# Seven block products for eight in the gated unit and the output projection of a hybrid attention and state-space layer

## The chip, the cores and the metric

The kernel runs on one core of a Trainium2 chip. Its engines are TensorE (PE in the rows; PEld is its loading of weights), VectorE (DVE), ScalarE (ACT), GpSimd (POOL) and SyncE (SP), which here does nothing but issue DMAs. The metric is the device time of one launch in microseconds, as the median of several executions; one further execution was taken with the hardware profiler, and all rows below are from that one.

## What is computed

One layer of an encoder, 1024 tokens of width 2048, all in fp32. The part in question stands in the middle (cut from the reference; `y_attn`, `y_ssm`, `gate_s` come from the input projection, attention and the scan):

```
y_ssm = gelu(y_ssm)
glu   = y_ssm @ w_glu + b_glu                      # 1024 x 1024 by 1024 x 2048
y_ssm = glu[..., :1024] * sigmoid(glu[..., 1024:]) * silu(gate_s)
h     = x + concatenate([y_attn, y_ssm]) @ w_out   # 1024 x 2048 by 2048 x 2048
gate  = sigmoid(rms_norm(h) @ w_ple_gate)          # 2048 x 2048
h     = h + gate * (p @ w_ple_proj)
out   = rms_norm(h)
```

## The kernel before

All matrices lie with channels on the 128 partitions and tokens along the free axis. Every fp32 product is made of three matmuls: each operand is split into a high part H (rounded to fp32r, by ACT) and a low part L (what the rounding left, by DVE), and H H + H L + L H is summed in PSUM. `split` does that (L307 on ACT, L308 on DVE; with a gain L310 and L311), `split_pool` does both on POOL.

The stages follow each other on PE: the input projection with the scan of the state-space part beside it (to 966 us), attention (to 1219), and then `back`, once for each half of 512 tokens. A half consists of the gated unit (names `gv`, `gg`: 8 pairs of output tiles, 8 blocks of input channels each), the output projection (`ph`: 16 tiles by 16 blocks) and the gate with the projection of p (`pg`: 16 by 16, `pp`: 16 by 2). `mm_half` issues the three matmuls of a block, 128 x 128 weights by 128 x 512 tokens. Its weights come four blocks at a time: `w_dma` loads 128 x 512 into `wraw` (3 buffers) on SP's queue, `w_split` splits it into `wH` and `wL` (4 buffers), and `w_next` keeps this two groups ahead of PE. All weights of `back` are loaded and split twice, once for each half.

The order on each engine is the order in which the program writes the instructions; nothing is reordered. What has to run beside the matmuls is written as a generator and put into `bgs`; each `tick` (after every second block) lets every generator go one step. So `fin_glu` (L1094 to L1096) evacuates a pair of tiles, `fin_h` (L1105 to L1116) adds x to a tile of the projection, splits it at once as an operand of the gate, and adds its square to `xsq`, on POOL (L1114). Operands of a stage are kept split in SBUF, in tiles of 128 x 2 x 512 from the pool `big` (33 buffers).

Of the kernel before, what the change touches and what calls it, by code (L numbers as in the profile page):

```python
# [16 lines left out]
SEQ = 1024  # L17
# [221 lines left out]
class Kernel:  # L239
# [10 lines left out]
    def __init__(self, ctx, tc, ins, out):  # L250
# [13 lines left out]
        self.bgs = []  # L264
# [5 lines left out]
    def tick(self):  # L270
        for g in list(self.bgs):
            try:
                next(g)
            except StopIteration:
                self.bgs.remove(g)

    def drain(self):
        while self.bgs:
            self.tick()
# [79 lines left out]
    def w_plan(self):  # L359
# [10 lines left out]
        for kind, n in self.order[2:]:  # L370
            tile_(w_in[self.COL[kind] + n], KD)
        for _ in range(2):
            for n in range(8):
                tile_(self.i["w_glu"][n], 8)
                tile_(self.i["w_glu"][n + 8], 8)
            for n in range(16):
                tile_(self.i["w_out"][n], 16)
# [22 lines left out]
    def w_next(self):  # L400
        n = self.wi
        while len(self.w_raw) < min(n + self.W_DMA + 1, len(self.wq)):
# [3 lines left out]
        while len(self.w_hl) < min(n + self.W_SPLIT + 1, len(self.wq)):  # L406
            self.w_split()
# [3 lines left out]
        return r  # L411

# [28 lines left out]
    def scratch(self):  # L441
# [11 lines left out]
        self.d_h = [[d(f"d_h{f}_{n}", (128, 512)) for n in range(KD)] for f in range(2)]  # L453
# [449 lines left out]
    def attn_scores(self, b):  # L903
        nc, sm = self.nc, self.sp
# [117 lines left out]

    def mm_half(self, ps, nk, xs):

        nc = self.nc
        for k in range(nk):
            if k % 4 == 0:
                H, L = self.w_next()
            while k not in xs:
                assert self.bgs  # L1030
                self.tick()
            x = xs[k]
            nc.tensor.matmul(ps, H[:, k % 4], x[:, 0], start=(k == 0), stop=False)  # L1033
            nc.tensor.matmul(ps, H[:, k % 4], x[:, 1], start=False, stop=False)  # L1034
            nc.tensor.matmul(ps, L[:, k % 4], x[:, 0], start=False, stop=(k == nk - 1))  # L1035
# [3 lines left out]
    def y_load(self, hf, js=range(8)):  # L1039
        raw = []  # L1040
        for j in js:
            t = self.cyc()
            self.nc.sync.dma_start(
                t.rearrange("p (t c) -> p t c", t=4),
                self.d_y[j][4 - 4 * hf : 8 - 4 * hf].rearrange("t f c -> f t c"),
            )
            raw.append(t)
        return raw

    def y_gelu(self, raw):  # L1050
        for t in raw:
            self.nc.scalar.activation(t, t, AF.Gelu_apprx_tanh)

    def y_first(self, raw):
        for _ in range(8):
            yield
        self.y_gelu(raw)

    def y_split(self, hf, raw, yg, j0=0, pool=False):
# [356 lines left out]
```

## Time and profile before

| | us |
|---|---|
| median of three runs | 2173.71 (2167.40 to 2174.03) |
| profiled execution, its own time | 2165.21 |
| its span, first to last instruction | 2163.3 |
| TensorE busy | 2112.9 |
| VectorE busy | 1358.0 |
| ScalarE busy | 787.9 |
| GpSimd busy | 618.1 |

The profiled execution lies 8.5 us under the median of the runs, and 1.9 us of its time lie outside the span. Busy times of PE are modelled from pipelined matmuls, so they are to be read with the starts of the matmuls beside them.

### The profile page before, as it was taken

The numbers are of one execution on the slowest core, as the hardware profiler recorded it, in microseconds if no ns is written. First come the engines' busy times: TensorE is split into PE (matmuls) and PEld (weight loads), VectorE is DVE, ScalarE is ACT, GpSimd is POOL, SyncE is SP. The second block draws the span as 40 slices with busy tenths as digits, with TensorE's granted clock in tenths as the row PEclk, the third lists the DMA queues.
The fourth block names the chain that finished last, engine by engine and source line by source line (L and its number), as shares of the span: only waits on it lengthen the run. The fifth ranks groups of instructions, "written<-read, shape, count | busy, mean of one in ns | idle before, by whom it ended". The sixth has DMA issues, their size and how long they took to land.

```text
span 2163.3 us, 29094 instructions
## 1 busy us (share of the span) xinstructions
PE 2112.9 (98%) x10428; PEld 1765.6 (82%) x10428; DVE 1358.0 (63%) x2274; ACT 787.9 (36%) x1429; POOL 618.1 (29%) x605
## 2 busy tenths in 40 slices
PE   8999999999999999999999999999999999999996
PEld 6888878888878887778989888888888788888885
DVE  7654787778888787838999644444444744444334
ACT  7111322222222222337777633333335433333332
POOL 0143456555556565502113000111121001111122
PEclk9999999999999999999999999999999999999998
DMA  6323233332332332341111334444434744443333
GB/s 215 96 95 102 81 87 101 90 94 86 95 99 77 88 105 72 100 157 65 70 41 40 122 122 137 145 154 122 125 122 144 235 128 145 146 152 109 128 113 126
DMA packets 171151, 245.06 MB, mean 113 GB/s; under 512 B 27136, under 2 KB 77440, under 8 KB 170752
## 3 DMA queue, kind: packets, MB, share of 16 engines
q1 hardware_dynamic: 169856, 241.12, 35.9%
q10 hardware_dynamic: 1152, 2.10, 0.3%
q8 instruction: 82, 1.34, 0.2%
q14 instruction: 61, 0.50, 0.1%
HBM read 189.35 MB, written 48.56 MB: 110 GB/s over the span
## 4 chain that ended last, share of the span: by engine, by line
PE 50%; DVE 3%; ACT 1%; issue 1%; DMA 1%; POOL 0%; DVEq 0%; SPq 0%; ACTq 0%
PE ph L1035 5%; PE ph L1033 5%; PE ph L1034 5%; PE pg L1035 5%; PE pg L1033 5%; PE pg L1034 5%; PE ptr L943 2%; PE pv L956 1%; PE pv L957 1%; PE pv L958 1%; PE S L913 1%; PE gg L1035 1%; PE S L916 1%; PE S L912 1%; PE gg L1033 1%; PE gg L1034 1%
## 5 line engine op out<-in xcount | busy, mean ns | idle before, releaser
L308 DVE TENSOR_TENSOR wL<-wraw,wH 128x512 fp32r<-128x512 f32 (+1 forms) x496 | 402.6, 832 | 445.3 <-ACT wH L307 440.0
L307 ACT CAST wH<-wraw 128x512 fp32r<-128x512 f32 (+1 forms) x496 | 292.7, 604 | 443.5 <-PE ph L1034 125.8
L1033 PE MATMUL pg<-hg,wH 128*128 128x512 f32 x512 | 200.3, 391 | 0.0
L1035 PE MATMUL pg<-hg,wL 128*128 128x512 f32 x512 | 199.5, 390 | 0.6 <-DVE wL L308 0.6
L1034 PE MATMUL pg<-hg,wH 128*128 128x512 f32 x512 | 199.2, 389 | 0.0
L1114 POOL TENSOR_TENSOR xsq<-xsq,tz 128x512 f32<-128x512 f32 x30 | 39.0, 1301 | 515.9 <-ACT tz L1113 515.9
L825 ACT COPY ks<-kp 16x224 f32<-16x224 f32 x32 | 10.7, 336 | 341.7 <-DVE ks L824 189.4
L1035 PEld LDWEIGHTS pg<-hg,wL 128*128 128x128 f32 x512 | 96.1, 188 | 21.4 <-DVE wL L308 1.3
L1034 PEld LDWEIGHTS pg<-hg,wH 128*128 128x128 f32 x512 | 96.1, 188 | 20.5 <-issue 0.5
L1033 PEld LDWEIGHTS pg<-hg,wH 128*128 128x128 f32 x512 | 96.1, 188 | 20.1 <-issue 0.5
L507 PE MATMUL zga<-hH,wH 128*128 128x512 f32 x256 | 104.0, 406 | 0.0
L507 PE MATMUL zgs<-hH,wH 128*128 128x512 f32 x256 | 102.5, 401 | 0.7 <-ACT wH L307 0.7
L507 PE MATMUL zq<-hH,wH 128*128 128x512 f32 x256 | 102.9, 402 | 0.0
L508 PE MATMUL zga<-hL,wH 128*128 128x512 f32 x256 | 100.2, 392 | 0.0
L508 PE MATMUL zq<-hL,wH 128*128 128x512 f32 x256 | 100.2, 391 | 0.0
L508 PE MATMUL zgs<-hL,wH 128*128 128x512 f32 x256 | 100.0, 391 | 0.0
L1033 PE MATMUL ph<-ma,wH 128*128 128x512 f32 x256 | 99.6, 389 | 0.0
L1034 PE MATMUL ph<-ma,wH 128*128 128x512 f32 x256 | 99.6, 389 | 0.0
L1035 PE MATMUL ph<-ma,wL 128*128 128x512 f32 x256 | 99.6, 389 | 0.0
L1033 PE MATMUL ph<-ms,wH 128*128 128x512 f32 x256 | 99.6, 389 | 0.0
L1034 PE MATMUL ph<-ms,wH 128*128 128x512 f32 x256 | 99.6, 389 | 0.0
L1035 PE MATMUL ph<-ms,wL 128*128 128x512 f32 x256 | 99.6, 389 | 0.0
(420 smaller groups left out, 5356.0 us busy)
## 6 DMA issues: line engine op xcount, KB each, us to landing
wraw<-in_w_in_dram SPq DMA_DIRECT2D x144, 256.0 KB
wraw<-in_w_out_dram SPq DMA_DIRECT2D x128, 256.0 KB
wraw<-in_w_gate_dram SPq DMA_DIRECT2D x128, 256.0 KB
wraw<-in_w_glu_dram SPq DMA_DIRECT2D x64, 256.0 KB
xraw<-in_xT_dram SPq DMA_DIRECT2D x15, 512.0 KB
out_dram<-h SPq DMA_DIRECT2D x24, 256.0 KB
t<-zz SPq DMA_DIRECT2D x40, 128.0 KB
d_u<-tz SPq DMA_DIRECT2D x16, 256.0 KB
```

Of the source, the lines that this page charges most:

```text
L307: nc.scalar.copy(H, src)
L308: nc.vector.tensor_tensor(L, src, H.bitcast(F32), ALU.subtract)
L507: nc.tensor.matmul(ps[h], H[:, kk, :], rH[:, s], start=(k == 0), stop=False)
L508: nc.tensor.matmul(ps[h], H[:, kk, :], rL[:, s], start=False, stop=False)
L912: nc.tensor.matmul(S[:, s], qH[:, qs], kH[:, s], start=True, stop=False)
L913: nc.tensor.matmul(S[:, s], qH[:, qs], kL[:, s], start=False, stop=False)
L916: nc.tensor.matmul(S[:, s], qL[:, qs], kH[:, s], start=False, stop=True)
L943: nc.tensor.transpose(pc[:, b], P[:, 512 * hf + 128 * b : 512 * hf + 128 * b + 128], self.ident)
L1033: nc.tensor.matmul(ps, H[:, k % 4], x[:, 0], start=(k == 0), stop=False)
L1034: nc.tensor.matmul(ps, H[:, k % 4], x[:, 1], start=False, stop=False)
L1035: nc.tensor.matmul(ps, L[:, k % 4], x[:, 0], start=False, stop=(k == nk - 1))
L1114: nc.gpsimd.tensor_tensor(acc, acc, s2, ALU.add)
```

## The change

The gated unit, the attention half of the output projection (its first 1024 input channels) and the state-space half become three stages of their own, each over all 1024 tokens. In each, the 1024 input channels are cut in two, the tokens in two, and the output tiles are taken in pairs: a 2 x 2 by 2 x 2 block product, done with Strassen's seven products in Winograd's order of sums. A stage is 8 units (`unit`), one for each pair of output tiles; a unit is 7 products of 4 blocks of 128 channels, each 3 matmuls, so 84 matmuls of the same shape as before. Each product has a PSUM tile of its own (`pr`) and is closed after 12 matmuls.

- Weights: a unit loads its four blocks once (`sw_dma`, `sraw`, 6 buffers), makes four sums of them on POOL (`sw_sum`, L436) and splits seven operands (`sw_prep`), two products ahead.
- Token operands: a stage has 7 sets of 4 tiles. Four sets are sums, made on POOL by `t_make` (16 operations a stage) and stored to DRAM (`d_t`): for the first stage in attention, for the second from the second unit of the first stage on, for the third from the first unit of the second stage on. `put` loads each tile raw into the slot of its own low part, and `fill` splits it in place some ticks later, one tile a tick. The 28 tiles of a next stage are loaded and split in the last unit of a stage and the first of the next, as products of that last unit free their slots.
- Evacuation: `u_glu` and `u_out` combine the seven products in fp32, with DVE reading PSUM and POOL adding to the token-wide tiles `cx`. The gated result goes to DRAM (`d_ms`), the partial sum of the projection too (`d_p`), and h (`d_h`), from which `put_h` loads the operands of the gate and splits them with the gain.
- GELU is applied to whole channels ahead of attention and stored (`y_prep`, `d_y2`). The gate stage itself keeps its matmuls; both of its halves now follow each other. `xsq`, the sum of squares of h, is 1024 wide, and the sums for the last norm move to other tiles.

The core of the diff:

```diff
-        while len(self.w_hl) < min(n + self.W_SPLIT + 1, len(self.wq)):
+        while len(self.w_hl) < min(n + self.W_SPLIT + 1, self.w_end):
+    def sw_sum(self, u, o, a, b, op):
+        if o not in self.sr and isinstance(o[1], str):
+            self.sr[o] = self.wp.tile([128, 512], F32, name="wraw", tag="wraw", bufs=3)
+        self.nc.gpsimd.tensor_tensor(self.sr[o], self.sr[a], self.sr[b], op)
+    def sw_prep(self, g):
+        u, i = divmod(g, 7)
...
+        src = (A11, A12, S2, A11, S1, A12, A22)[i]
...
+        self.split(H, L, self.sr[src].rearrange("p (k m) -> p k m", m=128))
+        self.shl[g] = (H, L)
+        if i == 0:
+            self.sw_dma(u + 1, (0, 1))
+        elif i == 1:
+            self.sw_sum(u, S1, A21, A22, ALU.add)
+            self.sw_sum(u, S2, S1, A11, ALU.subtract)
+        elif i == 2:
+            self.sw_sum(u, A11, A11, A21, ALU.subtract)
...
+        elif i == 3:
...
+            self.sw_sum(u, A12, A12, S2, ALU.subtract)
...
+        elif i == 4:
...
+            self.sw_dma(u + 1, (2, 3))
...
+    def sw_next(self):
+        g = self.sg
+        self.sg += 1
+        for j in range(g, g + 3):
+            if j not in self.shl:
+                self.sw_prep(j)
+        return self.shl.pop(g)
...
+    def put(self, X, key, src, gain=None, pool=False, wait=6):
+        x = self.hl("st")
+        self.nc.sync.dma_start(x[:, 1].bitcast(F32), src)
+        self.fq.append((self.nt + wait, X, key, x, gain, pool))
...
+    def unit(self, X, thread, hook):
+        nc = self.nc
+        next(thread)
+        for i in range(7):
+            H, L = self.sw_next()
+            ps = self.psC("pr")
+            for k in range(4):
+                while (i, k) not in X:
+                    assert self.fq
+                    self.tick()
+                x = X[i, k]
+                nc.tensor.matmul(ps, H[:, k], x[0], start=(k == 0), stop=False)
+                nc.tensor.matmul(ps, H[:, k], x[1], start=False, stop=False)
+                nc.tensor.matmul(ps, L[:, k], x[0], start=False, stop=(k == 3))
+                self.tick()
+            thread.send(ps)
+            hook(i)
...
+    def u_out(self, m, src, dst, sq):
...
+        ps = yield
+        u1 = self.t2k("tz")
+        nc.scalar.copy(u1, ps)
+        add(r[0], h0, u1)
+        ps = yield
+        done(r[0], h0, ps)
+        ps = yield
+        nc.vector.tensor_tensor(u1, ps, u1, ALU.add)
+        ps = yield
+        u2 = self.t2k("tz")
+        nc.vector.tensor_tensor(u2, ps, u1, ALU.add)
+        add(r[1], h1, u2)
+        add(r[1], h0, u2)
+        ps = yield
+        nc.vector.tensor_tensor(u1, ps, u1, ALU.add)
+        add(r[0], h1, u1)
+        done(r[1], h1, ps)
+        ps = yield
+        done(r[0], h1, ps)
...
+        ps = yield
+        done(r[1], h0, ps)
...
```

In it `add` is a sum on POOL, and `done` one on DVE from PSUM, with the square on ACT and its sum on POOL where the third stage needs them.

How the instructions stand on DVE where one stage passes into the next. Before, at the first tiles of the projection (`ph`) of a half; x4 means four in a row:

```order
L308 TENSOR_TENSOR ms_7_12660<-tz,ms_7_12660 128x512
L308 TENSOR_TENSOR wL<-wraw,wH 128x512 x4
L1105 TENSOR_TENSOR r_12636<-ph,r_12636 128x512
L311 SCALAR_TENSOR_TENSOR hg_0_12733<-r_12636,vec,hg_0_12733 128x512
L308 TENSOR_TENSOR wL<-wraw,wH 128x512 x4
L1105 TENSOR_TENSOR vr<-ph,vr 128x512
```

Now, in the last unit of the first stage, from its third product on (`st` are tiles of the next stage, split in place; `pr` is a product in PSUM):

```order
L311 TENSOR_TENSOR wL<-sraw,wH 128x512
L311 TENSOR_TENSOR st<-st 128x512 x4
L1209 TENSOR_TENSOR tz<-pr,tz 128x512
L311 TENSOR_TENSOR wL<-sraw,wH 128x512
L311 TENSOR_TENSOR st<-st 128x512 x4
L1212 TENSOR_TENSOR tq<-pr,tz 128x512
L1213 SCALAR_TENSOR_TENSOR tz<-pr,vec,tz 128x512
L311 TENSOR_TENSOR wL<-sraw,wH 128x512
L311 TENSOR_TENSOR st<-st 128x512 x4
L1217 TENSOR_TENSOR tz<-pr,tz 128x512
L1218 TENSOR_TENSOR cx<-tz,tq 128x512
L311 TENSOR_TENSOR wL<-sraw,wH 128x512
```

Where a weight split stood behind other weight splits and one operation on a finished tile, it now stands behind four splits of the next stage's tiles in each product.

On POOL, the projection before has one operation in a tile of 48 matmuls; the rows around it are those of the gate, ahead of it and behind it:

```order
L1151 TENSOR_TENSOR xsq<-xsq,tq 128x512
L1140 TENSOR_TENSOR h_14_15385<-tab,tz 128x512
L1114 TENSOR_TENSOR xsq<-xsq,tz 128x512 x15
L1140 TENSOR_TENSOR h_0_17674<-W,tz 128x512
L1140 TENSOR_TENSOR h_0_17674<-tab,tz 128x512
```

Now, one unit of the third stage (84 matmuls) on POOL, from the weight sums for it on (`sraw`, `wraw` are weights and their sums, `cx` the tiles of h):

```order
L436 TENSOR_TENSOR wraw<-sraw 128x512
L436 TENSOR_TENSOR wraw<-wraw,sraw 128x512
L1254 TENSOR_TENSOR xsq<-xsq,tq 128x512
L436 TENSOR_TENSOR sraw<-sraw 128x512
L1242 TENSOR_TENSOR cx<-cx,tz 128x512
L436 TENSOR_TENSOR sraw<-sraw,wraw 128x512
L1254 TENSOR_TENSOR xsq<-xsq,tq 128x512
L1242 TENSOR_TENSOR cx<-cx,tz 128x512 x3
L1254 TENSOR_TENSOR xsq<-xsq,tq 128x512 x2
```

The fifteen sums of a half's projection, one in 10.9 us, become twelve in every unit, and four of them stand between a load and a weight split.

## Rows read from the trace of the kernel before

**Rows 1.** The page, parts 1 and 2: busy us, share, instructions; tenths in 40 slices.
```profile
PE 2112.9 (98%) x10428; PEld 1765.6 (82%) x10428; DVE 1358.0 (63%) x2274; ACT 787.9 (36%) x1429; POOL 618.1 (29%) x605
...
ACT  7111322222222222337777633333335433333332
...
PEclk9999999999999999999999999999999999999998
```

**Rows 2.** Windows by stage; the first row names the columns.
```profile
core 0: us, PE busy (x) PEld busy (x) DVE busy (x) ACT busy (x) POOL busy (x), PEclk, DMA share, GB/s
...
100.00:740.00 640.00, 634.61 (x3191) 529.31 (x3190) 467.89 (x791) 151.72 (x342) 343.07 (x353) 1.00 0.31 93
740.00:1218.70 478.70, 461.34 (x2764) 399.76 (x2763) 387.46 (x684) 253.41 (x463) 148.35 (x141) 1.00 0.24 76
1218.70:1305.70 87.00, 87.00 (x387) 72.05 (x386) 41.59 (x63) 33.25 (x55) 0.00 (x0) 1.00 0.49 158
1305.70:1479.80 174.10, 174.10 (x770) 144.16 (x769) 78.33 (x99) 58.97 (x98) 18.21 (x14) 1.00 0.47 146
...
1672.00:1763.60 91.60, 90.61 (x401) 74.12 (x400) 56.45 (x92) 37.25 (x64) 3.89 (x3) 1.00 0.57 187
1763.60:1937.00 173.40, 173.40 (x767) 143.58 (x766) 78.53 (x99) 58.98 (x98) 18.22 (x14) 1.00 0.48 148
```

**Rows 3.** Tiles gv and ph, first half: ns min/median/max, first and last start.
```profile
L1033 PE MATMUL gv<-yg,wH x64: 389/389/396, 1218.8 to 1299.8; 128*128 128x512 f32 x64
...
L1033 PE MATMUL ph<-ma,wH x128: 389/389/389, 1305.9 to 1473.9; 128*128 128x512 f32 x128
...
L1035 PE MATMUL ph<-ms,wL x128: 389/389/389, 1311.8 to 1479.8; 128*128 128x512 f32 x128
```

**Rows 4.** Lines 308, 307, 1105, 1113 (1305.7 to 1479.8), 1114; DVE's 311 from 1218.
```profile
L308 DVE TENSOR_TENSOR wL<-wraw,wH x64: 677/693/1451, 1309.6 to 1477.9; 128x512 fp32r<-128x512 f32 x64
...
L307 ACT CAST wH<-wraw x64: 602/622/623, 1308.9 to 1477.3; 128x512 fp32r<-128x512 f32 x64
...
L1105 DVE TENSOR_TENSOR W<-ph,W x4: 691/692/692, 1349.6 to 1458.4; 128x512 f32<-128x512 f32 x4
...
L1113 ACT ACTIVATE tz<-W x4: 616/616/618, 1351.0 to 1459.8; 128x512 f32<-128x512 f32 x4
...
L1114 POOL TENSOR_TENSOR xsq<-xsq,tz x30: 1290/1297/1338, 1330.0 to 1945.6; 128x512 f32<-128x512 f32 x30
...
L311 DVE SCALAR_TENSOR_TENSOR hg<-W,vec,hg 128x512 fp32r<-128x512 f32 x8 | 6.0, 752 | 6.3 <-ACT hg L310 6.3
```

**Rows 5.** Timelines of POOL and DVE in the projection: start us, us.
```profile
1438.78 1.30 POOL L1114 TENSOR_TENSOR xsq<-xsq,tz 128x512 f32<-128x512 f32 x1 [9.58 <-ACT tz L1113]
...
1439.18 1.45 DVE L308 TENSOR_TENSOR wL<-wraw,wH 128x512 fp32r<-128x512 f32 x1 [0.28 <-ACT wH L307]
...
1442.58 0.69 DVE L308 TENSOR_TENSOR wL<-wraw,wH 128x512 fp32r<-128x512 f32 x1 [1.35 <-ACT wH L307]
```

**Rows 6.** Scan stage: line 699 overall; POOL and DVE timelines at 514 to 521.
```profile
L699 POOL TENSOR_TENSOR tab<-tab,ot x32: 1282/1620/1631, 195.5 to 916.6; 128x512 f32<-128x512 f32 x32
...
519.59 1.62 POOL L699 TENSOR_TENSOR tab<-tab,ot 128x512 f32<-128x512 f32 x1
...
515.04 0.67 DVE L594 TENSOR_TENSOR zz<-zz,rope_t 64x512 f32<-64x512 f32 x1
...
519.98 1.78 DVE L594 TENSOR_TENSOR zz<-zz,rope_t 64x512 f32<-64x512 f32 x1
```

**Rows 7.** Attention on DVE: line 947 among the groups, line 936 by source.
```profile
L947 DVE TENSOR_TENSOR PTL<-ptr,PTH 128x512 fp32r<-128x512 f32 x128 | 81.9, 681 | 2.4 <-ACT PTH L946 2.4
...
L936 DVE TENSOR_SCALAR P<-P,mx x64: 469/478/1258, 975.4 to 1213.0; 128x512 f32<-128x512 f32 x64
```

**Rows 8.** The busiest stretch for DMA: chain of waits, and its window.
```profile
1685.49 5.47 DMA r<-d_o
...
1703.23 4.36 DMA E<-d_o
...
1700.00:1712.00 12.00, 11.08 (x49) 8.76 (x48) 10.29 (x17) 5.42 (x10) 0.00 (x0) 1.00 0.82 262
```

**Rows 9.** PE's timeline in the scan stage, and the window behind it.
```profile
643.54 1.33 PE L787 MATMUL V<-U,WT 128*128 128x128 f32 x8 [2.06 <-ACT ys L873]
...
642.00:650.00 8.00, 6.46 (x28) 5.27 (x29) 6.08 (x9) 1.94 (x4) 4.91 (x7) 0.79 0.64 197
```

More of the change, by code (lines that the diff above doesn't have):

```diff
@@ L270, in tick @@
     def tick(self):
+        self.nt += 1
         for g in list(self.bgs):
@@ L275, in tick @@
                 self.bgs.remove(g)
+        if self.fq and self.fq[0][0] <= self.nt:
+            self.fill(*self.fq.pop(0)[1:])
     def drain(self):
-        while self.bgs:
+        while self.bgs or self.fq:
             self.tick()
@@ new lines, in y_prep @@
+    def y_prep(self, js, tiles):
+        nc = self.nc
+        for t, j in zip(tiles, js):
+            nc.sync.dma_start(t.rearrange("p (t c) -> p t c", t=8), self.d_y[j].rearrange("t f c -> f t c"))
+        for _ in range(5):
+            yield
+        for t in tiles:
+            nc.scalar.activation(t, t, AF.Gelu_apprx_tanh)
+        yield
+        yield
+        for t, j in zip(tiles, js):
+            nc.sync.dma_start(self.d_y2[j][:, 0:512], t[:, 512:1024])
+            nc.sync.dma_start(self.d_y2[j][:, 512:1024], t[:, 0:512])
@@ L1036, in mm_half @@
+            nc.tensor.matmul(ps, L[:, k % 4], x[0], start=False, stop=(k == nk - 1))
             if k % 2:
                 self.tick()
[L1039 to L1052, printed above, removed]
@@ L1118, in h_rstd @@
-    def h_rstd(self):
+    def h_rstd(self):
+        for _ in range(3):
+            yield
+        pc = self.colsum([self.xsq[:, self.half(h)] for h in range(2)])
+        yield
+        self.rsqrt(pc, DM, self.rk[:, 0:8])
+        dg = [self.spread(self.rk[:, 4 * h : 4 * h + 4]) for h in range(2)]
         yield
         yield
-        pc = self.colsum([self.xsq[:, 0:512]])
-        yield
-        self.rsqrt(pc, DM, self.rk[:, 0:4])
-        dg = self.spread(self.rk[:, 0:4])
-        yield
-        yield
-        self.nc.vector.tensor_copy(self.xsq[:, 0:512], self.rows(dg))
@@ L1129, in fin_g @@
-    def fin_g(self, hf, n, pg, pp, ho, hp):
+        for h in range(2):
+            self.nc.scalar.copy(self.xsq[:, self.half(h)], self.rows(dg[h]))
+    def fin_g(self, hf, n, pg, pp, ho, hp, acc):
         nc = self.nc
-        acc = self.xsq[:, 512:1024]
         t = self.t2k("tz")
-        nc.vector.tensor_tensor(t, pg, self.xsq[:, 0:512], ALU.mult)
+        nc.vector.tensor_tensor(t, pg, self.xsq[:, self.half(hf)], ALU.mult)
         nc.scalar.activation(t, t, AF.Sigmoid)
```

373 lines of the change are left out of this document (258 added, 115 removed).

## Prediction

> **What bounds the kernel now.** I read the page first. TensorE is busy for 2112.9 of 2163.3 us, VectorE (DVE) for 63%, GpSimd (POOL) for 29% [rows 1]; the granted clock is full almost to the end. The windows by stage say the same from the first gated unit on: in the stretches of the gated unit and of the projection PE is busy to within 1 us, while DVE does 42 to 79 us in stretches of 87 to 174 [rows 2]. So a matmul removed there comes off the time, unless another engine becomes late. A matmul's 389 ns are its latency; its pitch follows from starts: the projection of the first half starts at 1305.9 and its last matmul, the 768th, at 1479.8, so (1479.8 - 1305.9) / 767 = 0.2267 us. The gated unit ahead (384 matmuls, 1218.8 to 1305.9) gives 0.2268, although its groups close after 24 matmuls and those of the projection after 48 [rows 3]: shorter groups cost nothing, so I give groups of 12 the same pitch.
>
> **What is removed.** Gated unit and projection are 768 + 1536 = 2304 matmuls now. After, 24 units of 7 products of 12 make 2016. 288 x 0.2267 = **-65.3 us**. A unit of 84 is 19.04 us of PE, a product 2.72.
>
> **What is added, and where it lies.** The durations, each 128 x 512: the low half of a split on DVE 0.69 alone, the high half on ACT 0.62, a DVE operation that reads PSUM 0.69, a sum on POOL 1.29 to 1.30 [rows 4]. By counts none of the engines passes 19.04 us in an ordinary unit: in the third stage DVE has 14 operations (9.7 us), ACT 12 (7.4 us), POOL 12 (15.5 us). But the two do not run side by side. A POOL sum runs from 1438.78 to 1440.08; a split on DVE that begins at 1439.18 takes 1.45, to 1440.63, which is 0.55 after POOL's end, and the next one that meets no sum takes 0.69 [rows 5]. In the scan stage both sides pay: POOL's last sum of a table takes 1.29 at best and 1.62 in the median, and beside it stands a DVE operation of 1.78 us whose form takes 0.67 alone [rows 6]. So sums on POOL and DVE operations with two SBUF inputs take turns; a POOL sum costs the pair 1.29 us, a split 0.55 (what is left of it behind the sum) to 0.69. DVE operations with a PSUM input are untouched: the PTL subtractions keep 0.68 in attention, where POOL is busy a third of the time [rows 2, 7]. Term by term, as low / taken / high:
>
> - Third stage, 8 units: 12 x 1.29 + 7 x (0.55 to 0.69) = 19.3 to 20.3 against 19.04, so 0.3 to 1.3 a unit: 2 / 6 / 10.
> - Second stage, while the operand sums of the third are made (units 0 to 3; four more sums a unit beside its 8, the same 12): three units outside the stage change: 1 / 2 / 4. Units 4 to 6, at 8 sums, fit (15 us). In the first stage 6 + 4 sums and 9 SBUF operations are 17.9 to 19.1: nothing.
> - Change from the first stage to the second. 28 tiles are split in the last unit and the first of the next, four a product for six products in a row, where DVE also has a weight split and one or two PSUM operations a product. Over the two units the pair has 18 sums and 44 SBUF operations: 23.2 + 24.2 to 30.4 = 47.4 to 53.6 against 38.1. Weights are split two products ahead; 5.44 + 0.45 (the low half is the third matmul) - 1.31 (ACT and DVE) leaves 4.6 us in hand. What is late next is a weight's low half, since it queues on DVE behind the four fills. Stall 9.3 to 15.5 less 4.6: 5 / 8 / 11.
> - Second to third: 20 sums, 42 SBUF operations: 48.9 to 54.8, less 38.1 and 4.6: 6 / 9 / 12.
> - Entry from attention: 12 fills, five weight splits, four sums and four PSUM operations in the first four products: 18 against 10.9 + 4.6: 0 / 2 / 5.
> - Exit to the gate. In the last unit 14 tiles of h are split with a gain. No row shows that form (two SBUF inputs and a scalar) beside POOL; the nearest, the plain split, takes turns. If it does, 14 x 0.75 [rows 4] joins 15.5 + 3.9 on the pair: 29.9, 10.8 above the unit, 6 behind the slack; if not, nothing: I take 3. Then the gate's first weights are split after the last product's 0.69 + 0.62 (evacuation, square) and 0.62 + 0.69 of their own, less 0.45: 2.2 us of idle PE. The third weight is queued on SP behind a store of h that SP waits for (loads took 4.4 and 5.5 us in the busiest stretch [rows 8]), 2 more if late: 2 / 7 / 10.
> - TensorE's clock. After an idle 2.06 us at 643.5 the granted clock is 0.79 over 642 to 650 [rows 9], so 0.21 x 8 = 1.7 us are lost to a stretch at 1.2 GHz. Gaps of that size stand at three stage changes: 0 / 3 / 7.
> - Attention: 16 more sums on POOL and four more pool splits. They can hit the scaling of P (0.48 alone, 1.26 at worst [rows 7]), 20 x 0.58 = 12 at most if each hits and DVE has no slack: 0 / 2 / 8.
>
> GELU on whole channels and its store (cover: ACT, two to three tenths busy in the last input tiles [rows 1]; eight of 1.2 us, 10 us, if bare), sums of the first stage in attention, and the round trips of partial sum and h (two units of lead) I take as hidden. The last operand's square, add and final norm are unchanged.
>
> Sum: 2 + 1 + 5 + 6 + 0 + 2 + 0 + 0 = 16 at the low end, 6 + 2 + 8 + 9 + 2 + 7 + 3 + 2 = 39 taken, 67 at the high end. Against the profiled execution's own 2165.2: 2165.2 - 65.3 + 39 = 2139. The median of the runs shown is 2173.7, 8.5 above; against it 2147. I forecast between, **2142 us**.
>
> One rule of the Trainium skill speaks for a larger loss. The row shows: the split that meets a running sum ends 0.55 us after it, 0.14 less than it takes alone [rows 5]. The page "SBUF — State Buffer", section "SBUF: two separate sides", holds that a GpSimd operation and a DVE operation with two SBUF inputs lock each other out for a whole instruction. The trace agrees on the turns, but by the rule a split costs its whole 0.69: the terms are then 10, 4, 11 and 12 in the first four lines and the sum 2151. With 0.55 in all of them they are 2, 1, 5 and 6 and the sum 2128. I took the middle, since in a full queue some splits start while POOL is idle.
>
> **The rivals.**
> - Nearly all hidden. Fills might find POOL idle: DVE alone has 44 SBUF and about 14 PSUM operations at 0.69 in the two units, 40 us against 38.1 + 4.6, and would fit. For it: POOL's sums wait for evacuations. Against: DVE's work is bunched in six products, 26 us for 16.3. Stalls of 0 to 15: 2100 to 2120.
> - The pair paces ordinary units. If a sum holds it for 1.62, as in the scan stage [rows 6], the third stage takes 12 x 1.62 + 4.8 = 24.3 a unit, 5.2 x 8 = 42 lost there, and some 10 more in the second; the chain behind it is S1, S2, split, product, and add, evacuation, square, add. 2160 to 2175. Against: in that stretch DVE was busy 73% of the time, 468 of 640 us [rows 2]; here it is half.
> - Slower, by DMA at the stage changes. 28 tiles of 256 KB are 7.3 MB, with weights and stores some 10 MB, wanted within 35 us. The fastest stretch of the trace moves 262 GB/s at 0.82 busy [rows 8]: 38 us, 3 lost per change. To cost the 65 us each change needs 35 + 33 = 68 us, 150 GB/s. SP issues in order, and ACT waits at its queue's head for each fill, so a slow load would hold weights too. Beyond that point it is slower: 2180.
> - The change buys less than 288 matmuls' time, if pitch grows with groups of 12: two equal pitches speak against it.
>
> **How the numbers follow.** Forecast (stalls 16 to 52, up to 2158 with the runs' spread) 0.52; nearly hidden 0.20; pair paces 0.20; slower by DMA 0.06; longer pitch 0.02. The range leaves out the fastest part of the second and the slowest of the others: 2110 to 2170; the forecast's own is 2116 to 2158. A change of 0.3% (6.5 us, bounds 2167 and 2180) is what a measurement here can tell. Faster: 0.52 + 0.20 + half of 0.20 = 0.82; same: 0.08 + 0.02 = 0.10; slower: 0.02 of the third case and 0.06 = 0.08.
>
> **What would show it.** 2016 matmuls pr from first to last start in 457 us plus idle time; PE gaps that end on DVE wL in the last unit of a stage and the first of the next, hardly any in the middle units; DVE split means near 1.2 in the third stage and 0.69 where POOL is idle; POOL at 80% there; a gap of 2 us ahead of pg, released by ACT. It is wrong if PE's gaps end on DMA st, if POOL releases gaps in every unit, or if the pitch within a product is above 0.23.

## The result, and the profile after

The changed kernel takes **2208.82 us** (median of 4 runs, 2206.17 to 2212.11), the kernel before beside it 2173.87 (2167.4 to 2176.54): ratio 1.0166, 95% interval 1.014 to 1.0192. It is slower, by 1.7%; the forecast was 2142 in a range of 2110 to 2170, with a chance of 0.08 for this side. The profiled execution took 2209.37 us.

The page of the profile after, busy times and the granted clock in 40 slices, beside [rows 1]:

```profile
PE 2093.2 (95%) x10140; PEld 1725.1 (78%) x10140; DVE 1484.1 (67%) x2394; ACT 798.6 (36%) x1454; POOL 961.1 (44%) x837
...
PEclk9999999999999999999999999889999999999998
```

The 288 matmuls are gone (10428 instructions became 10140), yet PE's busy time fell by 19.7 us only and its share from 98 to 95%. The windows, for [rows 2] (units of 84 matmuls in the three stages, then the gate; PE's window counts run over by a few):

```profile
core 0: us, PE busy (x) PEld busy (x) DVE busy (x) ACT busy (x) POOL busy (x), PEclk, DMA share, GB/s
1225.60:1249.80 24.20, 20.47 (x89) 15.50 (x88) 19.60 (x28) 12.66 (x23) 6.12 (x5) 1.00 0.61 214
...
1270.30:1293.80 23.50, 21.24 (x86) 16.77 (x85) 14.21 (x17) 5.97 (x10) 17.55 (x13) 0.93 0.59 201
...
1335.20:1373.30 38.10, 38.10 (x170) 31.56 (x169) 25.59 (x33) 11.51 (x20) 18.39 (x13) 1.00 0.43 140
1373.30:1394.30 21.00, 19.79 (x88) 16.06 (x86) 18.36 (x27) 11.78 (x22) 6.74 (x4) 1.00 0.74 257
1394.30:1425.10 30.80, 24.13 (x82) 18.12 (x83) 27.15 (x34) 13.98 (x27) 15.05 (x10) 0.83 0.60 215
1425.10:1503.30 78.20, 64.89 (x254) 50.54 (x253) 32.09 (x41) 13.59 (x24) 51.11 (x38) 0.91 0.62 208
...
1561.90:1581.80 19.90, 19.31 (x86) 15.55 (x85) 14.11 (x22) 11.25 (x22) 7.13 (x5) 1.00 1.02 361
1581.80:1612.80 31.00, 22.29 (x86) 17.00 (x85) 26.22 (x34) 12.86 (x26) 20.21 (x11) 0.89 0.57 204
1612.80:1735.60 122.80, 119.27 (x505) 93.13 (x504) 70.93 (x84) 40.93 (x72) 103.74 (x72) 1.00 0.46 150
1735.60:1766.50 30.90, 23.64 (x88) 17.92 (x87) 24.22 (x29) 16.16 (x28) 18.80 (x14) 0.86 0.59 211
1766.50:1790.00 23.50, 20.37 (x81) 15.47 (x82) 12.24 (x28) 11.19 (x19) 2.44 (x2) 0.89 0.59 184
...
1970.00:2040.00 70.00, 63.77 (x253) 49.06 (x252) 39.00 (x67) 26.75 (x45) 9.67 (x8) 0.93 0.58 189
```

Two units that nothing disturbs (1335.2 to 1373.3) take 38.1 us: 19.05 each, PE never idle, clock 1.00. The price of a product is as forecast. Everywhere else in the list PE waits, and the clock is below 1.00 in seven of these eleven stretches, where [rows 2] had 1.00 in all. Units 1 to 3 of the second stage take 78.2 us for 57.1, with POOL busy for 51.1 of them and DVE for 32.1: neither is full. The chain that ended last, in order of time at the start of that stretch, says who is late:

```profile
1428.63 1.30 POOL t L1133
...
1429.95 0.32 SPq L1138
...
1430.32 2.49 DMA d_t<-t
...
1432.88 0.32 SPq L1124
...
1433.25 0.42 SPq L1124
...
1433.73 0.42 SPq L1183
...
1434.19 7.84 DMA cx<-in_xT_dram
...
1442.17 1.16 POOL cx L1242
...
1443.39 1.26 POOL sraw L436
```

POOL ends the last of four operand sums; SP, which had stood at its store (L1138), issues it; the store takes 2.49 us to land, and only then can SP load the next set into the same buffers (L1124). Behind that load in SP's order stands the load of x for this unit, issued 9 us after the unit began and landed 7.84 us later. POOL's addition into it (L1242) stands ahead of a weight sum (L436) in POOL's order, the weight's split waits for the sum, and the matmul for the split. In all, POOL waited 21.1 us for these loads in three waits.

### The profile page after: what moved, and what is told of

It is laid out like the page before. It is cut to its first block, busy times and chain, and to the rows that moved or that the text cites. A ratio compares the mean times of both kernels' runs of the same rounds, so it can differ in the third digit from the quotient of the medians.

```text
span 2207.6 us, 29212 instructions
## 1 busy us (share of the span) xinstructions
PE 2093.2 (95%) x10140; PEld 1725.1 (78%) x10140; DVE 1484.1 (67%) x2394; ACT 798.6 (36%) x1454; POOL 961.1 (44%) x837
## 5 line engine op out<-in xcount | busy, mean ns | idle before, releaser
L311 DVE TENSOR_TENSOR wL<-wraw,wH 128x512 fp32r<-128x512 f32 (+1 forms) x352 | 303.1, 878 | 368.1 <-ACT wH L310 366.3
L1174 PE MATMUL pr<-st,wL 128*128 128x512 f32 x672 | 274.6, 409 | 35.3 <-DVE wL L311 35.2
L1172 PE MATMUL pr<-st,wH 128*128 128x512 f32 x672 | 268.9, 400 | 12.2 <-ACT wH L310 12.2
L1173 PE MATMUL pr<-st,wH 128*128 128x512 f32 x672 | 267.7, 398 | 0.0
L1291 PE MATMUL pg<-st,wH 128*128 128x512 f32 x512 | 203.7, 398 | 9.1 <-ACT wH L310 7.7
L1292 PE MATMUL pg<-st,wH 128*128 128x512 f32 x512 | 202.4, 395 | 0.6 <-DVE st L314 0.6
L1293 PE MATMUL pg<-st,wL 128*128 128x512 f32 x512 | 201.6, 394 | 0.7 <-DVE wL L311 0.7
L1174 PEld LDWEIGHTS pr<-st,wL 128*128 128x128 f32 x672 | 130.1, 194 | 81.7 <-DVE wL L311 55.5
L1172 PEld LDWEIGHTS pr<-st,wH 128*128 128x128 f32 x672 | 130.5, 194 | 40.7 <-ACT wH L310 15.1
L1173 PEld LDWEIGHTS pr<-st,wH 128*128 128x128 f32 x672 | 129.9, 193 | 28.2
L311 DVE TENSOR_TENSOR wL<-sraw,wH 128x512 fp32r<-128x512 f32 x120 | 119.1, 993 | 39.1 <-ACT wH L310 38.5
L1242 POOL TENSOR_TENSOR cx<-cx,tz 128x512 f32<-128x512 f32 x64 | 97.0, 1531 | 107.6 <-DVE tz L1266 45.6
L1291 PEld LDWEIGHTS pg<-st,wH 128*128 128x128 f32 x512 | 97.4, 190 | 32.1 <-ACT wH L310 9.3
L1292 PEld LDWEIGHTS pg<-st,wH 128*128 128x128 f32 x512 | 97.6, 191 | 23.1 <-DVE st L314 2.5
L1293 PEld LDWEIGHTS pg<-st,wL 128*128 128x128 f32 x512 | 97.4, 190 | 22.8 <-DVE wL L311 2.5
L765 POOL TENSOR_TENSOR tab<-pa 128x512 f32<-128x512 f32 x32 | 41.3, 1292 | 156.5 <-DVE r L900 156.5
```

What stands on the lines that cost most here:

```text
L311: nc.vector.tensor_tensor(L, src, H.bitcast(F32), ALU.subtract)
L765: gp.tensor_tensor(out, x[:, :, None, :].to_broadcast(sh), pw[:, :, :, None].to_broadcast(sh), ALU.mult)
L1172: nc.tensor.matmul(ps, H[:, k], x[0], start=(k == 0), stop=False)
L1173: nc.tensor.matmul(ps, H[:, k], x[1], start=False, stop=False)
L1174: nc.tensor.matmul(ps, L[:, k], x[0], start=False, stop=(k == 3))
L1242: nc.gpsimd.tensor_tensor(x[:, h], x[:, h], u, ALU.add)
```

## The experiments

Each run is told by its median, its ratio to the kernel before on the same chip, and the length of the three stages in its profiled execution, from the starts of the first matmuls pr (the third up to the first pg). Without a stall a stage is 152.3. Gains in us are differences of medians. The kernel before took 2173.9 us beside the kernel after and 2169.8 to 2171.9 beside the experiments, so a gain against the kernel after is 2 to 4 us smaller by the ratios.

| run | us | ratio (95%) | first | second | third |
|---|---|---|---|---|---|
| after | 2208.8 | 1.0166 (1.014 to 1.0192) | 168.7 | 187.6 | 184.6 |
| e1 | 2183.5 | 1.0061 (1.0044 to 1.0078) | 159.7 | 170.1 | 184.4 |
| e2 | 2188.2 | 1.0077 (1.0053 to 1.01) | 165.2 | 170.8 | 185.2 |
| e3 | 2180.1 | 1.0046 (1.0031 to 1.0061) | 159.4 | 169.3 | 185.2 |
| e4 | 2190.0 | 1.009 (1.0069 to 1.0111) | 168.0 | 177.4 | 179.2 |
| e5 | 2171.5 | 1.0002 (0.9991 to 1.0013) | 160.1 | 169.3 | 173.8 |
| e6 | 2186.2 | 1.0061 (1.0045 to 1.0078) | 156.3 | 172.3 | 191.3 |
| e7 | 2176.9 | 1.0025 (1.0016 to 1.0035) | 160.5 | 164.0 | 185.3 |
| e8 | 2184.6 | 1.0054 (1.0039 to 1.0069) | 159.9 | 169.3 | 184.4 |
| e9 | 2169.4 | 0.9993 (0.9981 to 1.0004) | 159.6 | 164.0 | 177.0 |
| e10 | 2169.4 | 0.9982 (0.9969 to 0.9995) | 159.7 | 165.3 | 174.1 |
| e11 | 2169.7 | 0.9998 (0.9985 to 1.0011) | 160.1 | 165.4 | 170.2 |
| e12 | 2171.5 | 1.0004 (0.9993 to 1.0015) | 160.4 | 161.9 | 181.9 |
| e13 | 2139.8 | 0.9862 (0.9843 to 0.9882) | 158.3 | 155.9 | 156.5 |
| e14 | 2168.0 | 0.9992 (0.998 to 1.0003) | 158.6 | 164.0 | 169.7 |
| e15 | 2174.9 | 1.0028 (1.0013 to 1.0043) | 164.3 | 169.2 | 169.1 |
| e17 | 2168.3 | 0.9987 (0.9977 to 0.9996) | 155.5 | 165.1 | 170.5 |
| e18 | 2164.4 | 0.9967 (0.9955 to 0.998) | 157.1 | 165.0 | 170.7 |

**e1, a gap around the stores.**
```diff
-            yield
-            yield
+            for _ in range(8):
+                yield
             for i in range(4):
                 self.nc.sync.dma_start(self.d_t[s][k][i], b[i])
+            for _ in range(8 if s else 0):
+                yield
...
-                        self.bg(self.t_make(1, src, self.four_sm, 20))
+                        self.bg(self.t_make(1, src, self.four_sm, 8))
...
-                    self.bg(self.t_make(2, self.d_ms, self.four_sm, 20))
+                    self.bg(self.t_make(2, self.d_ms, self.four_sm, 8))
```


> Changes only where the making of the operand sums stands in SP's order: eight steps between the last sum and the four stores, eight between the stores and the reload of the same buffers, in place of the 20 behind the loads. The sums, the splits and the bytes are the same. Theory A (SP stands at the head of its queue for a store to land, and the loads of x behind it are late): units 1 to 3 of the second stage, now 30.0, 24.9 and 23.3 us, come to 19 to 21 each, unit 0 to 26 to 29, and the time to 2180 to 2192. Rival B (POOL and DVE taking turns is the limit there, the prediction's own cause): nothing they do is taken away, so these units stay within 1 us and the time at 2204 to 2213.

25 us come back (23 by the ratios), and the windows of units 0 to 2 of the second stage show where:

```profile
1385.80:1421.60 35.80, 26.64 (x84) 19.46 (x85) 31.73 (x34) 13.58 (x26) 22.83 (x15) 0.81 0.59 213
1421.60:1440.60 19.00, 19.00 (x86) 15.73 (x85) 11.97 (x14) 4.74 (x8) 16.12 (x12) 1.00 0.78 261
1440.60:1459.70 19.10, 19.10 (x86) 15.82 (x85) 11.61 (x14) 4.73 (x8) 16.16 (x13) 1.00 0.80 275
```

Units 1 to 3 run without a stall (57.0 us with 36 sums on POOL, for 78.2 with 38), with the same splits, nearly the same bytes, and 261 to 275 GB/s for the 208 of the kernel after. So POOL and DVE taking turns was not their limit; SP's order was. The first stage gains 9 us in the same way (8 of them in units 1 to 4, beside the making of the other operand sums). Unit 0 went the other way, 35.8 for an expected 26 to 29: the set's four sums now fall into it (15 sums on POOL for 10).

**e2 and e3, the addend a unit earlier.** In e2 alone, in e3 with the edit of e1:
```diff
-        next(thread)
         for i in range(7):
+            if i == 3 and nxt:
+                next(nxt)
```


> Loads the addend of a unit (x, the partial sum, or the gate input gs) at the fourth product of the unit before, not at the unit's own start. Theory A (the addend's late landing holds POOL, and through POOL's and DVE's order the weight splits): the first units of the second and third stage (30.8 and 31.0) lose 4 to 7 us each, units 1 to 3 of the second stage 10 to 18 together, and the time is 2178 to 2192. Rival B (POOL and DVE taking turns, or the stage's own tiles landing late): the first units keep 28 or more and the time is 2200 to 2212.

> Both edits together. If they cure the same wait twice (theory A, one chain), the gain is that of the better one and 0 to 5 us more: 2172 to 2188. If they act on different waits the gains add: 2150 to 2172. Under rival B (turns of POOL and DVE) no change: 2200 to 2212.

e2 gains 21 us (19 by the ratios): units 1 to 3 of the second stage take 21.0, 20.8 and 20.9 us. The first units stay at 32.0 and 30.8, so what holds those is not the addend. Together the edits are 3.4 us better than e1: one chain, cured twice.

**e4, no low halves at the two changes.**
```diff
-            self.split(x[:, 0], x[:, 1], x[:, 1].bitcast(F32), gain)
+            self.nc.scalar.copy(x[:, 0], x[:, 1].bitcast(F32))
```


> Leaves out the low half of the split of the 56 tiles at the two stage changes (DVE does not subtract, so the low parts of these operands are wrong and the output is not the reference's); loads, high halves and matmuls stay. 28 DVE operations of 0.69 us a change. The prediction's cause (DVE and POOL taking turns behind the fills, 8 and 9 us a change) expects the last unit of a stage and the first of the next to fall from 51.8 and 51.0 us together to 40 to 44, and the time to 2186 to 2195. Theory A (late landings) expects under 4 us a change: 2202 to 2212.

19 us (16 by the ratios). Last unit and first of the next together fall from 51.8 to 41.3 at the first change and from 51.0 to 45.4 at the second; units 1 to 3 of the second stage keep 29.2, 26.8 and 23.8. So the kernel after has both: DVE's splits of the next stage's tiles at the changes, where the forecast had its stalls, and SP's order behind them.

**e5, e6, e9: the third stage's ordinary units (20.4 us).** e5 leaves out POOL's addition of the squares (30 of them; the expectation says 31), e6 gives the weights a lead of three products, e9 (on e7, below) does the addition on DVE:
```diff
-                nc.gpsimd.tensor_tensor(acc, acc, s2, ALU.add)      # e5
-        for j in range(g, g + 3):                                   # e6
+        for j in range(g, g + 4):
-                nc.gpsimd.tensor_tensor(acc, acc, s2, ALU.add)      # e9
+                nc.vector.tensor_tensor(acc, acc, s2, ALU.add)
```


> Built on the kernel with store gap and prefetch (2180.1). Leaves out POOL's addition of the squares of h in the third stage (31 sums; the final norm is wrong, the output is not the reference's). Ordinary units of the third stage take 20.4 to 20.5 us there. Theory P (POOL and DVE have no room: 12 sums a unit at 1.3 to 1.7) expects 19.0 to 19.3 with 8 sums a unit, 2166 to 2172 in all. Theory C (the chain S1, S2, split, product is too long for a lead of two products, wherever POOL stands) expects the stalls ahead of the third and the fifth product to stay: 20.0 to 20.5 a unit, 2176 to 2181.

> Built on the kernel with store gap and prefetch (2180.1). Weights are summed and split three products ahead, not two; nothing else. Theory C (lead too short for the chain) expects ordinary units of the third stage at 19.0 to 19.3 for 20.4, and 2 to 3 us less in the first units of the second and third stage (36.0, 30.9): 2160 to 2170. Theory P (POOL and DVE full) expects 20.2 to 20.5 as before and 2176 to 2182.

> Built on the kernel with store gap, prefetch and the operand sums one unit later (2176.9). The addition of the squares in the third stage goes from POOL to DVE; nothing is left out. If POOL and DVE take turns, a sum on DVE costs the pair 0.6 to 0.7 in place of 1.3: third-stage units of 20.4 come to 19.0 to 19.2, 2166 to 2170. If DVE itself were the limit, they would rise to 21 or more and the time to 2180 or more.

Windows over six ordinary units of the third stage, one row each of e5, e6 and e9:

```profile
1591.00:1705.20 114.20, 114.20 (x506) 94.56 (x505) 66.57 (x84) 39.52 (x73) 69.70 (x50) 1.00 0.48 162
```
```profile
1584.20:1713.00 128.80, 120.70 (x505) 92.71 (x504) 73.95 (x84) 40.27 (x73) 102.80 (x72) 1.00 0.42 143
```
```profile
1584.90:1699.60 114.70, 114.49 (x504) 94.33 (x504) 87.50 (x108) 39.32 (x72) 72.41 (x50) 1.00 0.47 161
```

With 8 sums on POOL a unit takes 19.0, with 12 it takes 20.4, and a longer lead makes it 21.7 (why worse is not settled). Done on DVE, 24 more operations there, the same additions cost next to nothing that PE sees: DVE is busy for 87.5 us of 114.7, and units take 19.1. So the additions of the squares on POOL are what costs these units 1.4 us each. That the pair has no room for 12 sums is not shown by it, for units 1 to 3 of the second stage in e1 have 12 sums and 7 splits a unit as well, and lose nothing:

```profile
1421.80:1478.80 57.00, 57.00 (x253) 47.22 (x252) 36.19 (x41) 14.23 (x24) 48.49 (x36) 1.00 0.79 270
```

At the prediction's prices 36 sums and 21 splits are 58.0 us (a split at 0.55) to 60.9 (at 0.69). ACT's squares are not the reason, for they stay in e5. What differs in the third stage is the place of the additions: each waits for ACT's square of a tile that DVE has just evacuated, and the weight sums of the next products stand behind it in POOL's order. The waits of the kernel after over its six ordinary units:

```profile
POOL xsq L1254 <- ACT tq L1253: 5.3, 12, 1.9
PE pr L1174 <- DVE wL L311: 3.5, 12, 0.6
```

e5 and e9 take away the additions' time and their place together, so how much of the 1.4 us belongs to which stays open.

**e7 and e10, POOL's sums off the first units.** e7 (on e3) starts the making of the third stage's operand sums one unit later; e10 (on e9) moves the additions into the addends to DVE (and one of them a product later).
```diff
-                if u == 0 and s == 1:                               # e7
+                if u == 1 and s == 1:
-            nc.gpsimd.tensor_tensor(x[:, h], x[:, h], u, ALU.add)   # e10
+            nc.vector.tensor_tensor(x[:, h], x[:, h], u, ALU.add)
```


> Built on the kernel with store gap and prefetch (2180.1). The operand sums of the third stage are begun one unit later, so that four of POOL's sums leave the first unit of the second stage (36.0 us, where DVE's fills run 1.3 to 1.7 us each beside them). If POOL and DVE taking turns sets that unit: 31 to 33 us and 2173 to 2177 in all. If the fills' number on DVE alone does, or late tiles: 35 to 36 and 2178 to 2182.

> As the run with the squares on DVE, and the additions of combined products into the addends (4 a unit in the second and third stage) go from POOL to DVE too. Turns: the first units of the second and third stage (30.7 and 31.1), where four fills on DVE took 6.8 us beside POOL's three additions, fall to 22 to 27, the last unit of the third with its gap (31.6) to 25 to 29: 2150 to 2162. If the number of DVE operations is the limit there (some 60 of 0.69 in two units): no gain or a loss, 2166 to 2180.

e7: unit 0 of the second stage falls from 36.0 to 30.7, 1.3 for each of four sums. In the third stage's unit 0 of e7 stands what the prediction spoke of, timelines of DVE and POOL:

```profile
1553.84 6.82 DVE L311 TENSOR_TENSOR st<-st 128x512 fp32r<-128x512 f32 x4
1560.59 0.68 DVE L1248 TENSOR_TENSOR cx<-pr,cx 128x512 f32<-128x512 f32 x1
1561.19 0.68 DVE L311 TENSOR_TENSOR wL<-sraw,wH 128x512 fp32r<-128x512 f32 x1
```
```profile
1548.06 7.01 POOL L1245 TENSOR_TENSOR cx<-cx,tz 128x512 f32<-128x512 f32 x3 [8.74 <-DVE tz L1269]
1555.03 1.74 POOL L436 TENSOR_TENSOR wraw<-sraw 128x512 f32<-128x512 f32 x1
1556.85 1.59 POOL L436 TENSOR_TENSOR wraw<-wraw,sraw 128x512 f32<-128x512 f32 x1
```

Four fills take 1.7 each beside POOL's sums (0.69 alone, [rows 4]), then one evacuation, and only then the weight's low half, for which PE waited 4.9 us. But e10, which takes the additions away from POOL, gains 2.4 us in that unit and 0.3 in the second stage's, and nothing in the median: 2169.4, where turns expected 2150 to 2162. In the first units DVE is full with and without turns (e12 below): a sum that moves there takes a turn away and adds an operation.

**e8 and e11, the gate's first weights.** e8 (on e3) loads them up to two products earlier and splits them one earlier, e11 (on e10) splits the first two products earlier, ahead of the last squares.
```diff
-                if s == 2 and i == 5:                               # e11
+                if s == 2 and i in (3, 4):
                     self.w_end = len(self.wq)
                     self.w_dma()
-                    self.w_dma()
-                elif s == 2 and i == 6:
+                    if i == 4:
+                        self.w_split()
+                elif s == 2 and i == 5:
                     self.w_split()
```


> Built on the kernel with store gap and prefetch (2180.1). The gate's first weights are loaded two products earlier and split ahead of the last two evacuations; nothing else. If the gate's entry waits for these weights (TensorE is idle 4.86 us ahead of it, released by ACT's high half, which stands behind the last squares): the last unit with the gap falls from 31.6 to 25 to 28 and the time to 2173 to 2177. If it waits for the last evacuation, square and tile of h instead, under 1 us: 2178 to 2182.

> As the run with squares and additions on DVE, and the gate's first weight is split two products earlier, ahead of the squares and evacuations of the last products on ACT. If ACT's order (a square that waits for a late evacuation stands ahead of that split) sets the gap ahead of the gate: 2 to 5 us below that run. If the late tile of h does, within 1 us of it.

e8 gains nothing: the last unit with its gap is 31.0 (31.6 in e3). The split is queued on ACT behind a square that waits for an evacuation, itself late behind fills on DVE; from the waits of e8 at 1711 to 1752:

```profile
ACT tq L1256 <- DVE cx L1248: 13.6, 5, 6.6
...
PE pg L1294 <- ACT wH L310: 4.0, 1, 4.0
```

With the split ahead of it (e11) that unit falls from 31.4 (e10) to 26.0 in the profile, but the median does not move; its gate is 4 us longer and its first unit of the third stage 1.6. Where the rest goes is not settled.

**e12, the weight sums on DVE too.**
```diff
-        self.nc.gpsimd.tensor_tensor(self.sr[o], self.sr[a], self.sr[b], op)
+        self.nc.vector.tensor_tensor(self.sr[o], self.sr[a], self.sr[b], op)
```


> As the run with squares and additions on DVE, and the weights' operand sums (4 a unit) on DVE too, so that POOL has only the sums of data operands. Turns alone: POOL is out of the way, but DVE has 26 operations, 17.9 of 19.04 us, in a unit of the third stage and nothing left at the stage changes; 5 us below to 10 us above that run. If turns were not the cause (each engine simply as long as its own work), DVE is the fullest of all kernels and the time 10 to 30 us above it.

2.1 us worse than e10: third-stage units are 20.3 again, and POOL, with nothing to do there, can't be the reason; DVE is busy for 98.35 us of 120 in them. Four sums of the unit on POOL and eight on DVE is the better share. The first units of the second and third stage, with next to no sum on POOL, show the changes without turns:

```profile
1392.50:1421.00 28.50, 20.62 (x83) 14.97 (x84) 26.61 (x43) 13.81 (x26) 1.10 (x1) 1.00 0.63 224
1554.50:1582.60 28.10, 22.12 (x85) 16.50 (x84) 25.45 (x43) 11.92 (x22) 0.00 (x0) 0.94 0.65 237
```

DVE is busy there for 26.6 and 25.5 us with 43 operations, 0.6 each. In the kernel after 34 operations, with POOL's sums beside them, took it 27.2 and 26.2 us, and the units 30.8 and 31.0. So the number of operations alone fills DVE at a change; turns make each longer.

**e13, no low halves at all** (changes and exit; on e11, the edit of e4 with the gain).

> Built on the run with adds on DVE and the gate's early split (2169.7). Leaves out the low half of the split of all tiles at the two stage changes and the exit (72 DVE operations; the output is not the reference's). If the number of these splits holds DVE there, the first units (30.4, 30.0) come to 19 to 22 and the last one with its gap (26.0) to 21 to 23: 2140 to 2150. If something else does (landing of tiles, evacuation, clock), less than half of that: 2158 to 2168.

30 us less than e11: 2139.8 beside a forecast of 2142, but only with these 72 operations left out. Windows of the last unit of the first stage, the first and the last of the second, and the last of the third with its gap:

```profile
1363.50:1383.50 20.00, 19.78 (x88) 16.05 (x86) 11.39 (x14) 11.91 (x22) 5.83 (x5) 1.00 0.66 236
1383.50:1406.10 22.60, 20.09 (x83) 15.17 (x84) 17.29 (x21) 14.58 (x27) 10.38 (x7) 1.00 0.83 301
1519.80:1539.40 19.60, 19.60 (x88) 16.22 (x88) 12.23 (x18) 12.27 (x22) 4.28 (x4) 1.00 1.00 355
...
1676.10:1695.90 19.80, 19.61 (x86) 15.61 (x85) 12.98 (x22) 15.53 (x26) 2.31 (x2) 1.00 0.73 266
```

The mean granted clock of the run is 0.992, for 0.986 in e11, 0.980 in the kernel after and 0.994 before: with the stalls most of the slow clock goes. So DVE's low halves hold the changes and the exit.

**e14 and e15, the same splits moved.** e14 (on e11) loads and splits the first tiles of the next stage a unit earlier; e15 also splits two of the four operand sums when they are made and stores both halves.
```diff
-                if u == 7:                                          # e14
+                if u == 6:
                     before()
+                    x = hl[n - 4] = self.hl("st")                   # e15
+                    self.split(x[:, 0], x[:, 1], b[n - 4])
```


> Built on the run with adds on DVE and the gate's early split (2169.7). The first four tiles of the next stage (five of h at the exit) are loaded and split one unit earlier, in the buffers that are free then. If DVE's splits hold the changes, four of 28 less there is 3 us a change at 0.69 each, 4 to 5 with what stands beside POOL: 2158 to 2165. If not, 2167 to 2172.

> As the run with four tiles earlier, and two of the four operand sums of each set (8 of the 28 tiles of a change) are split when they are made, in ordinary units, and stored as two halves; at the change they are only loaded, with twice the bytes (2.1 MB more a change). If DVE's splits hold the changes: first units at 22 to 25, 2148 to 2158. If DMA is near its limit there (0.70 busy at the first change), the added bytes eat it: 2158 to 2170.

Both miss. e14: 1.6 us, the first units keep 30.4 and 29.6; the five tiles of h now crowd the seventh unit (23.7). e15 is 6.8 worse than e14. In the profile that loss lies in the ordinary units in which the operand sums are made: 20.3 us in three units of the first stage and 20.1 to 20.8 in four of the second, for 19.0 in e14. The first unit of the second stage is still 30.2, but by another wait, shown by its windows and its waits there:

```profile
1391.00:1395.00 4.00, 3.33 (x14) 2.11 (x12) 1.11 (x1) 0.00 (x0) 3.42 (x3) 1.00 1.03 420
1395.00:1399.00 4.00, 0.00 (x0) 0.00 (x0) 0.00 (x0) 0.62 (x1) 0.00 (x0) 0.90 1.04 406
```
```profile
ACT st L310 <- DMA st<-d_o: 10.5, 1, 10.5
...
PE pr L1188 <- ACT wH L310: 7.2, 2, 6.9
```

In the second of these windows DVE and POOL are idle, the DMA engines are busy throughout at 406 GB/s, and ACT stands at its queue's head for a tile, with a weight's high half behind it. That is the mechanism of the DMA rival; it appears when some of DVE's splits leave the change and the bytes are raised.

**e16, the kernel before once more.**

> The kernel before, profiled a second time, for its first gated-unit matmul, at 1218.9 us in the first profile. If the change's work in input and attention costs the 7 to 13 us that all variants show there, it comes at 1217 to 1221 again; if the first profile was a quick one, at 1223 or later.

```profile
L1033 PE MATMUL gv<-yg,wH x128: 389/389/396, 1224.5 to 1767.4; 128*128 128x512 f32 x128
```

Its run took 2169.5 us; in the first profile (2165.2) this matmul stood at 1218.8 [rows 3]. The first product starts at 1226.2 in the kernel after and at 1223.1 to 1232.6 in the variants. So of the 7.4 us of the kernel after, 5.6 lie between the two profiles of the kernel before as well. From the first score matmul to there, attention takes 251.9 and 253.4 in those two, 254.6 in the kernel after and 255.2 to 259.6 in the variants, which leaves the change 1 to 8 us.

**e17 and e18, the lead of three again,** on e11 and on e14, now that POOL has four sums in a unit.

> Built on the run with adds on DVE and the gate's early split (2169.7), weights summed and split three products ahead. If the weight's low half behind a bunch of splits is what reaches TensorE, the first units (30.4, 30.0) come to 24 to 28 and ordinary units stay at 19.0: 2158 to 2165. If DVE has no room over the whole change, the same loss comes one product later: 2167 to 2172, and if POOL's order is what made the lead fail, units of the third stage rise over 20.

> As that run, and the first four tiles of the next stage one unit earlier (2168.0 without the lead). If both slacks act on the same queue, 2 to 5 us below the run with the lead alone; if the early tiles only shift the crowd (the seventh unit of the third stage then took 23.7), within 2 us of it.

Ordinary units stay at 19.0, so the lead no longer hurts, and the first stage gets 4.6 us shorter; the first units stay at 31.8 and 29.3 (e17), so DVE has no room over the whole change, as the second branch of the expectation had it. e18, with both, is 3.9 us below e17, though their runs overlap, and 6.4 us below the kernel before: ratio 0.9967 over five runs, the fastest kernel here that leaves nothing out.

## Why the prediction was wrong

Point by point, from the profiled execution; excess over 19.04 a unit, and how long PE was idle in it.

| step | low / taken / high | measured |
|---|---|---|
| 288 matmuls | -65.3 | as said (38.1 us for two undisturbed units) |
| third stage steady | 2 / 6 / 10 | 8.6 in six units, 1.4 each (122.8 for 114.2); the other two stand in the changes |
| second stage, units 1 to 3 | 1 / 2 / 4 | 21.1, and 1.4 in unit 4 |
| first stage, units 1 to 4 | nothing | 9.2, of which SP's order 8 |
| change first to second | 5 / 8 / 11 | 13.7 (21.0 + 30.8 - 38.1), idle 7.9 |
| change second to third | 6 / 9 / 12 | 12.8 (19.9 + 31.0 - 38.1), idle 9.3 |
| entry | 0 / 2 / 5 | 5.2, idle 3.7 |
| exit to the gate | 2 / 7 / 10 | 11.9 (30.9 - 19.0), idle 7.3 |
| clock | 0 / 3 / 7 | inside the rows above and below |
| attention and ahead | 0 / 2 / 8 | 7.4 by the first profile of before, 1.7 by the second |
| the gate | nothing | 21.7 (440.5 from the first pg to the end, 198.7 + 220.1 in two pieces before) |

The rows add up to 113 us where 39 were taken. The kernel before had 3.4 us of stalls of its own in its gated units and projections; 113 - 65.3 - 3.4 is 44.3, the difference of the two spans (2207.6 and 2163.3).

**The step that failed** is the term for the second stage (1 / 2 / 4), which counted only sums and splits and put the DMAs of the operand sums at nothing: the prediction takes "the round trips of partial sum and h" as hidden, and the round trips of the operand sums stand nowhere in its sum. They are 16 loads and 16 stores in each of the first two stages, on the queue that also brings the addends and weights, and a reload into the buffers just stored holds the whole queue until the store has landed. It cost 25 us by e1 (23 by the ratios). The prediction had seen that SP issues in order, but only priced it where many tiles move, at the stage changes. This step alone doesn't make the miss: with it cured e1 still takes 2183.5 us. The next two terms are most of the rest.

**The clock was mis-sized.** A stretch at half speed (1.2 GHz) was taken as one per change, 1.7 us. The rows after give 0.17 x 30.8 + 0.09 x 78.2 + 0.11 x 31.0 + 0.14 x 30.9 + 0.07 x 23.5 for the units, 0.11 x 23.5 + 0.07 x 70 for the gate: 29 us for the 3 taken, part of it while PE was idle anyway. At the two changes and the exit PE's idle time alone is 7.9, 9.3 and 7.3 us, for 8, 9 and 7 taken, and the slow stretches come on top: 8 and 0.17 x 30.8 = 5.2 are 13.2 for the 13.7 measured, 9 and 3.4 are 12.4 for 12.8, 7 and 4.3 are 11.3 for 11.9. So the stalls there were sized right and their clock was not. That they were sized so closely is luck in part, for the price rested on turns of POOL and DVE, and e12 has 28.5 and 28.1 us in the first units with next to no sum to take turns with.

**The gate was left out.** Its two halves stand back to back now; around 2000 us 16 tiles of h, the stores of the first half and the weights pass SP. From 1970 to 2040 PE is idle for 6.2 us, and 3.5 of them end on the high half of a gate weight, whose load ACT waits for:

```profile
ACT wH L310 <- DMA wraw<-in_w_gate_dram: 24.0, 8, 5.2
...
PE pg L1291 <- ACT wH L310: 3.5, 2, 2.7
```

From 1766 to 1790 PE is idle for 3.1 us. ACT waits there for gate weights too, but PE's longest gap ends on the scale of the norm, which DVE works out:

```profile
ACT wH L310 <- DMA wraw<-in_w_gate_dram: 8.4, 1, 8.4
...
PE bc L358 <- DVE tq L352: 2.6, 1, 2.6
```

The clock's share in the two stretches is 4.9 and 2.6 us: with the idle time some 17 of the 21.7. That the loads are late because of what stands ahead of them on SP is read from the order of the queue; no run here moved them.

**What held.** The pitch of groups of 12. The turns of POOL and DVE, in the durations of their operations (the rows of e7). The 20.4 us of the third stage's units were forecast at the upper end (12 x 1.29 + 7 x 0.69 = 20.3), but that is luck in part: the same sum holds for units 1 to 3 of the second stage, and once SP's order was cured they took 19.0 (e1). On the rule of the Trainium skill ("SBUF — State Buffer", "SBUF: two separate sides"), that one of the two blocks the other for a whole instruction: the trace agrees on the blocking (a sum of 4.09 us beside four splits, below), but as a sum over a unit the whole 0.69 is right in the third stage and too much in the second. Of the rivals, DMA at the changes was not the limit in the kernel after (e4, e13), and became it in e15. "The pair paces ordinary units" named 2160 to 2175 by 24.3 a unit; they took 20.4.

## What to carry to other kernels

When a step is added in the background, follow its DMAs through the queue that issues in order: a store and a reload of the same buffer put a round trip ahead of everything behind them, and some steps of other work between the two gave some 25 us here. Count bursts, not units: 28 splits at a stage change kept PE idle for 8 to 9 us though DVE was a third idle on average. Add to the stalls on TensorE the slow clock that may come with them (up to 29 us here), and before a sum is given to POOL beside DVE, ask whether DVE has room for it: it takes 0.69 us there for 1.29, and POOL's other work does not stand behind it.

## What the runs showed that was not expected

- The DMA engines moved 406 to 420 GB/s at the first change (the rows of e15 above), where the prediction took 262 at 0.82 busy [rows 8] as the fastest. The Trainium skill ("SBUF — State Buffer", the table of doors in "SBUF: two separate sides") gives about 436 GB/s for the DMA side, and the trace stays 4 to 7 per cent below it.
- The clock does not answer to idle time alone: unit 0 of the first stage has 3.7 us of idle PE and 1.00, unit 2 has 2.3 and 0.93; six units of the third stage with 3.5 us of idle in small pieces kept 1.00.
- In e13 the last unit of the second stage moved 355 GB/s and PE was never idle: so many bytes are no stall by themselves.
- Who waits in the turns of POOL and DVE changes within a few us. In e7 one of POOL's sums took 4.09 us beside four splits of DVE that took 2.49 together, as they do alone; five us later four splits beside POOL's sums took 6.82 (above).

```profile
1548.06 4.09 POOL L1245 TENSOR_TENSOR cx<-cx,tz 128x512 f32<-128x512 f32 x1 [8.74 <-DVE tz L1269]
```
```profile
1548.49 2.49 DVE L311 TENSOR_TENSOR st<-st 128x512 fp32r<-128x512 f32 x4
```
